# Summing a one-number-per-partition verdict: a one-column matmul against a GpSimd reduction, inside a matmul-bound kernel

## The chip, the cores and the metric

The kernel runs on one core of a Trainium2 chip. The metric is device time in microseconds (us), as a median of several executions. Engines are named as the profile names them: PE is TensorE (PEld its weight loads), DVE is VectorE, ACT is ScalarE, POOL is GpSimd, SP is SyncE.

## The reference

```python
batch, seq, dim, hidden = 16, 256, 512, 2048
def reference(x, w1, w2):
    h = x @ w1                              # 4096x512 @ 512x4096
    gate, value = np.split(h, 2, axis=-1)
    h = np.maximum(gate, 0) * value
    return (h @ w2).astype(np.float32)      # 4096x2048 @ 2048x512
```

## The kernel before

The kernel computes both matmuls in float16 with a seven-product (Strassen-like) scheme. This is only safe if the inputs have a normal scale. So the kernel sums squares of pieces of the inputs into a table `st` of 128 partitions by 152 columns, and during the last of its four second matmuls it judges the table. If every entry is between two bounds, a flag is 0 and the kernel ends; otherwise it does everything again in a general way. The steps that the change touches are these:

```python
    def judge():                                   # VectorE
        n = st.shape[1]
        ok = wpool.tile([P, n], F32, name="ok")
        fit = wpool.tile([P, 2], F16, name="fit")
        nc.vector.tensor_scalar(out=ok, in0=st, scalar1=HIGH, scalar2=None, op0=LE)
        nc.vector.scalar_tensor_tensor(out=ok, in0=st, scalar=LOW, in1=ok, op0=GE, op1=MULT)
        nc.vector.memset(fit, 1.0)
        with nc.allow_low_precision("whole numbers below 2048"):
            nc.vector.tensor_reduce(out=fit[:, :1], in_=ok, axis=mybir.AxisListType.X, op=ADD)
        return fit

    def count(fit):                                # TensorE, then VectorE
        n = P * st.shape[1]
        ps = psx.tile([P, TH], F32, name="X", tag="X")
        nc.tensor.matmul(ps[:1, :1], fit[:, :1], fit[:, 1:], start=True, stop=True)
        nc.vector.tensor_scalar(out=flag, in0=ps[:1, :1], scalar1=n - 0.5, scalar2=None, op0=LT)
# ... cut ...
            # the last second matmul is a stream of 112 steps, two matmuls each;
            # job(u, f) puts f ahead of step u
            job(18, lambda: verdict.append(judge()))
            job(46, lambda: count(verdict[0]))
            job(78, lambda: verdict.append(nc.values_load(flag[0:1, 0:1], ...)))   # every engine reads the flag
```

The other party in the story is a sum of two operands on VectorE, done sixteen times in the last stream. TensorE waits for these sums:

```python
    def sum_of(o, n, eng=nc.vector):
        i0, i1, op = SUMS_X[n]
        eng.tensor_tensor(o[n], o[i0], o[i1], op=op)     # 128x1024 float16, both inputs in SBUF
```

## Time and profile before

| | before |
|---|---|
| median time (first three runs) | 307.98 us |
| span of the profiled run | 305.6 us |
| TensorE busy | 300.7 us, 98% |
| VectorE, ScalarE, GpSimd busy | 77%, 58%, 49% |
| chain that ended last | 96% TensorE |
| one product of eight 128x256 matmuls | every 0.87 us |
| the product that holds the count | 1.08 us |

These lines are from the page of the kernel before: span, busy times, the granted clock in tenths in 40 slices, and the chain of waits that ended last.

```profile
span 305.6 us, 5338 instructions
PE 300.7 (98%) x1933; PEld 187.0 (61%) x1933; DVE 236.0 (77%) x388; ACT 176.5 (58%) x348; POOL 151.2 (49%) x189
PEclk9999999999999999999999999999999999999999
PE 96%; DMA 1%; SPq 0%; POOL 0%; ACT 0%; issue 0%
```

Nearly all of the span is TensorE, at full clock. Time is only gained where TensorE works less or waits less.

Next is the timeline of the kernel before around the count. The columns are start, duration, engine, line, operation and count of merged instructions; the bracket tells how long the engine was idle and what released it.

```profile
286.90 0.60 PE L369 MATMUL Y<-v_T,w_stage 128*128 128x256 f16 x4
287.43 0.08 PEld L675 LDWEIGHTS <-fit 128*1 128x1 f16 x1 [0.21 <-issue]
287.43 0.16 PE L675 MATMUL X<-fit 128*1 128x1 f16 x1
287.53 0.61 PE L369 MATMUL Y<-v_T,w_stage 128*128 128x256 f16 x4
287.71 0.14 DVE L676 TENSOR_SCALAR flag<-X 1x1 int32<-1x1 f32 x1
287.98 1.04 PE L369 MATMUL W<-w,w_stage 128*128 128x256 f16 x8
```

The starts matter here, since the ends of matmuls are modelled and overlap. From 286.90 to 287.98 us is 1.08 us, where a product takes 0.87 us. So the count costs TensorE 0.21 us. Ordinary weight loads start about 0.1 us ahead of their matmul; the load of `fit` starts together with it.

The listing by tile of the kernel before shows who reads the flag, and when ("first to last start" after the durations; the rows of the other engines' sequencers are left out).

```profile
L783 POOLq TENSOR_LOAD <-flag x1: 491/491/491, 287.9 to 287.9; - x1
L783 PEldq TENSOR_LOAD <-flag x1: 488/488/488, 292.6 to 292.6; - x1
```

The flag is ready at about 287.85 us. TensorE's sequencer only asks for it at 292.6 us.

### The profile page before, as it was taken

What the parts mean: (1) busy time and instruction counts of PE and PEld (TensorE: products, weight loads), DVE (VectorE), ACT (ScalarE), POOL (GpSimd) and SP (SyncE); (2) the same over time, 40 slices, a digit from 0 to 9 for tenths busy, and PEclk for the clock granted to TensorE, in tenths of its full rate; (3) what the DMA queues carried; (4) which work ended last, traced back from release to release, by engine and by line L of the source; (5) the groups of instructions that cost most, each with busy time, mean ns of one, the idle gap of its engine ahead of it and who ended that gap; (6) DMA issues with size and microseconds to landing.
All of it is one profiled execution on the core that took longest, in us unless ns stands there. A gap on an engine that the chain in (4) does not pass through costs nothing.

```text
span 305.6 us, 5338 instructions
## 1 busy us (share of the span) xinstructions
PE 300.7 (98%) x1933; PEld 187.0 (61%) x1933; DVE 236.0 (77%) x388; ACT 176.5 (58%) x348; POOL 151.2 (49%) x189
## 2 busy tenths in 40 slices
PE   8999999999999999999999999999999999999995
PEld 6854545688844444478864444458884444447884
DVE  2779888899768898887537888888546888888851
ACT  2588886455955555538855555545866555553231
POOL 2399999800069999300029989800006998800000
PEclk9999999999999999999999999999999999999999
DMA  7977679954794170001354910000325110000133
GB/s 236 356 233 219 213 176 177 223 114 87 266 200 92 64 138 3 0 2 63 136 175 108 206 36 2 0 2 2 138 91 185 35 34 2 1 1 27 45 105 107
DMA packets 35838, 32.89 MB, mean 108 GB/s; under 512 B 14432, under 2 KB 31328, under 8 KB 35680
## 3 DMA queue, kind: packets, MB, share of 16 engines
q1 hardware_dynamic: 33536, 26.22, 28.7%
q0 software_dynamic: 2272, 6.29, 11.6%
q8 instruction: 16, 0.26, 0.3%
q14 instruction: 14, 0.11, 0.1%
HBM read 27.26 MB, written 12.58 MB: 130 GB/s over the span
## 4 chain that ended last, share of the span: by engine, by line
PE 96%; DMA 1%; SPq 0%; POOL 0%; ACT 0%; issue 0%
PE Y L256 26%; PE W L256 18%; PE X L256 18%; PE Y L369 14%; PE X L369 9%; PE W L369 9%; DMA w_stage<-in_w_dram 1%; PE W L332 1%; PE X L332 1%; PE Y L332 1%; PE Y L511 0%; PE X L511 0%; SPq L501 0%; POOL w_T L479 0%; SPq L222 0%; ACT o L417 0%
## 5 line engine op out<-in xcount | busy, mean ns | idle before, releaser
L256 PEld LDWEIGHTS <-w_T 128*128 128x128 f16 x524 | 51.1, 98 | 54.6 <-POOL w_T L237 0.9
L184 POOL TENSOR_TENSOR fold<-xh 128x1024 f32<-128x1024 f16 x16 | 30.3, 1896 | 94.6 <-DMA xh<-x 93.7
L256 PE MATMUL X<-x_A,w_B 128*128 128x512 f16 x248 | 73.7, 379 | 0.0
L256 PE MATMUL Y<-x_S,w_T 128*128 128x512 f16 x220 | 65.4, 379 | 0.0
L256 PEld LDWEIGHTS <-w_B 128*128 128x128 f16 x372 | 36.4, 98 | 42.0
L284 DVE SCALAR_TENSOR_TENSOR cc<-W,pu 128x512 f32<-128x512 f32 x62 | 42.9, 692 | 21.3 <-ACT pu L278 21.3
L264 ACT COPY Y<-X 128x512 f32<-128x512 f32 x62 | 35.4, 571 | 38.2 <-PE X L256 37.9
L278 ACT ACTIVATE pu<-Y 128x512 f32<-128x512 f32 x62 | 37.1, 598 | 33.9 <-PE Y L256 32.9
L187 POOL TENSOR_TENSOR fold<-fold 128x512 f32<-128x512 f32 (+2 forms) x96 | 51.8, 540 | 7.5
L369 PEld LDWEIGHTS <-w_stage 128*128 128x128 f16 x512 | 50.0, 98 | 5.8
L294 DVE SCALAR_TENSOR_TENSOR cc<-Y,pu 128x512 f32<-128x512 f32 x62 | 42.9, 691 | 6.6
L289 DVE SCALAR_TENSOR_TENSOR g<-X,cc 128x512 f16<-128x512 f32 x62 | 42.9, 691 | 2.3
L306 DVE SCALAR_TENSOR_TENSOR g<-Y,cc 128x512 f16<-128x512 f32 x62 | 42.3, 682 | 1.8 <-PE Y L256 1.8
L369 PEld LDWEIGHTS <-g 128*128 128x128 f16 x384 | 37.5, 98 | 8.2
L271 ACT ACTIVATE pu<-W 128x512 f32<-128x512 f32 x62 | 37.2, 600 | 0.8 <-PE W L256 0.6
L256 PE MATMUL W<-x_S,w_T 128*128 128x512 f16 (+1 forms) x152 | 36.9, 340 | 0.0
L256 PE MATMUL W<-x_S,w_B 128*128 128x512 f16 x124 | 36.9, 379 | 0.0
L256 PE MATMUL Y<-x_A,w_T 128*128 128x512 f16 x124 | 36.9, 379 | 0.0
L369 PE MATMUL X<-w,g 128*128 128x256 f16 x256 | 31.9, 273 | 0.0
L405 DVE SCALAR_TENSOR_TENSOR o<-W,pu 128x256 f32<-128x256 f32 x16 | 6.8, 423 | 21.0 <-PE W L369 21.0
L174 DVE TENSOR_TENSOR w_stage<-g 128x1024 f16<-128x1024 f16 x32 | 21.4, 685 | 0.2
L237 POOL TENSOR_TENSOR w_T<-w_stage 128x512 f16<-128x512 f32 (+1 forms) x16 | 18.7, 1173 | 2.6 <-DMA w_stage<-in_w_dram 2.5
(100 smaller groups left out, 306.7 us busy)
## 6 DMA issues: line engine op xcount, KB each, us to landing
w_stage<-in_w_dram SPq DMA_DIRECT2D x14, 512.0 KB, 6.0
out_dram<-o SPq DMA_DIRECT2D x26, 256.0 KB, 2.2
x<-in_x_dram POOLq DMA_DIRECT2D x4, 1024.0 KB, 10.5
xh<-x SPq DMA_DIRECT2D x16, 256.0 KB, 3.2
w<-in_w_dram POOLq DMA_DIRECT2D x2, 1024.0 KB, 10.0
out_dram<-o SPq DMA_DIRECT2D x12, 128.0 KB, 1.7
w_stage<-in_w_dram SPq DMA_DIRECT2D x4, 256.0 KB, 4.8
x_S<-in_x_dram SPq DMA_DIRECT2D x4, 256.0 KB, 5.7
```

The lines of the kernel that those rows point to most:

```text
L174: eng.tensor_tensor(o[n], o[i0], o[i1], op=op)
L184: nc.gpsimd.tensor_tensor(fold, t, t, op=MULT)
L187: nc.gpsimd.tensor_tensor(fold[:, :, :m], fold[:, :, :m], fold[:, :, m:2 * m], op=ADD)
L256: nc.tensor.matmul(ps[:, slice(*c)], wop[wn][:, b, self.jb * P:(self.jb + 1) * P], self.xo[xn][:, b, slice(*c)], start=fresh and b == c[0] ...
L264: nc.scalar.copy(out=self.Y, in_=self.X)
L271: nc.scalar.activation(self.p5, self.W, COPY, scale=GS)
L278: nc.scalar.activation(self.u2, self.Y, COPY, scale=GS)
L284: nc.vector.scalar_tensor_tensor(out=self.c12, in0=self.W, scalar=GS, in1=self.u2, op0=MULT, op1=ADD)
L289: nc.vector.scalar_tensor_tensor(out=self.g[:, self.jb, :TH], in0=self.X, scalar=0.0, in1=self.c12, op0=MAX, op1=MULT)
L294: nc.vector.scalar_tensor_tensor(out=self.c22, in0=self.Y, scalar=GS, in1=self.p5, op0=MULT, op1=ADD)
L306: nc.vector.scalar_tensor_tensor(out=self.g[:, self.jb, TH:], in0=self.Y, scalar=0.0, in1=self.c22, op0=MAX, op1=MULT)
L369: nc.tensor.matmul(ps, self.op[an][:, i], vop[wn][:, i], start=name in ("P1", "P5") and i == 0, stop=i == NJ // 2 - 1, skip_group_check=True)
```

## The change

The intent is to take the count from TensorE, which is the bottleneck, and give it to GpSimd, which is idle from 266.9 us on.

```diff
-        fit = wpool.tile([P, 2], F16, name="fit")
+        fit = wpool.tile([P, 1], F32, name="fit")
         ...
-        nc.vector.memset(fit, 1.0)
-        with nc.allow_low_precision("whole numbers below 2048"):
-            nc.vector.tensor_reduce(out=fit[:, :1], in_=ok, axis=mybir.AxisListType.X, op=ADD)
+        nc.vector.tensor_reduce(out=fit, in_=ok, axis=mybir.AxisListType.X, op=ADD)
@@ def count(fit):
-        ps = psx.tile([P, TH], F32, name="X", tag="X")
-        nc.tensor.matmul(ps[:1, :1], fit[:, :1], fit[:, 1:], start=True, stop=True)
-        nc.vector.tensor_scalar(out=flag, in0=ps[:1, :1], scalar1=n - 0.5, scalar2=None, op0=LT)
+        total = wpool.tile([1, 1], F32, name="total")
+        nc.gpsimd.tensor_reduce(out=total, in_=fit, axis=mybir.AxisListType.C, op=ADD)
+        nc.gpsimd.tensor_scalar(out=flag, in0=total, scalar1=n - 0.5, scalar2=None, op0=LT)
@@
-            job(46, lambda: count(verdict[0]))
+            job(18, lambda: count(verdict[0]))
```

## The prediction

> **What bounds the kernel.** TensorE. The page gives PE 300.7 us of a 305.6 us span (98%) at a granted clock of nine tenths or more in every slice, and the chain that ended last is 96% PE. VectorE is at 77%, ScalarE 58%, GpSimd 49%. Only what TensorE does, or waits for, costs time.
>
> **Where the change sits.** In the last second matmul. The timeline shows the verdict made on VectorE from 283.07 us (two compares, a memset of 0.06 us, a 0.31 us reduction ending at about 284.5 us). At 287.43 us TensorE does the one-column weight load (79 ns) and matmul (164 ns); VectorE compares at 287.71 us (0.14 us). The listing by tile shows who reads the flag: GpSimd's sequencer at 287.9 us, TensorE's at 292.6, ScalarE's at 293.4, VectorE's at 294.4, SyncE's at 295.2.
>
> **What is removed.** A product of eight matmuls goes by every 0.87 us (284.28, 285.16, 286.03, 286.90); the one with the count in it takes 1.08 us (286.90 to 287.98). So the count costs TensorE about 0.21 us, also seen as a 0.21 us "issue" gap before its weight load. This lies on the chain, so about 0.2 us comes back. VectorE loses 0.20 us (memset and compare), off the chain: it idles 1.3 to 2.1 us at a time here. One use of an X bank goes too; the next product into X starts at 294.09 us without a wait, so that gives nothing.
>
> **What is added.** On GpSimd, idle from 266.9 us on apart from its flag load: a sum of 128x1 over the partitions and a 1x1 compare. The trace has no sum over partitions. The Trainium skill ("GPSIMD Engine Reference", section "Cross-partition — where GPSIMD wins") states 247.7 us for 128x2048; no run here shows it yet. That is 0.12 us a column, if it goes column by column; with the 0.2 us of a small GpSimd instruction here (128x8 add, 203 ns) I estimate 0.5 to 3 us for the sum, say 1.5 us, and 0.1 to 0.2 us for the compare. The same page (section "Instruction dispatch") puts some 6 us on the first call into freshly loaded code; nothing shows that this needs it.
>
> **What of it is critical.** The sum can start at about 284.6 us. TensorE's sequencer asks for the flag at 292.6 us, and TensorE has queued work until about 294.5 us (the load sits inside the product that starts at 294.09 us). So sum plus compare may take about 8 us before the sequencer waits, about 9 before the matmuls do. At 1.5 us the flag comes at about 286.4 us, earlier than before. I expect no wait. GpSimd could hinder VectorE's 128x1024 sums that feed TensorE, but over the whole run these took 678 to 693 ns with GpSimd busy half the time, and the new instruction reads only 128 numbers.
>
> **Prediction.** 307.98 - 0.2 = 307.8 us; the runs of before alone scatter by 1 us. Range 307.1 to 308.7. Faster by over 2%: 0.01; within 2%: 0.92; slower by over 2%: 0.07.
>
> **What would show it right.** No one-column matmul; all products around 287 us 0.87 us apart; a GpSimd sum of 1 to 3 us starting near 284.6 us; no gap in PE after TensorE's flag load; the chain still 96% PE; the 128x1024 sums still 0.69 us.
>
> **What would make it wrong.** A sum with a fixed cost above 8 us (TensorE then stalls by the excess, one for one; over about 14 us it is 2% slower); a compare that reads the total too early, so that the general way runs and the time jumps by far more; or a long GpSimd instruction that holds VectorE's sums back.

## The result, and the profile after

The first measurement gave 308.37 us (307.63 to 308.71, 6 runs) for the changed kernel and 307.86 us (307.52 to 308.58, 6 runs) for the kernel before. The ratio is 1.0006, 95% interval 0.9987 to 1.0026: the same. A ratio is the mean time of one kernel's fast runs over that of the other's of the same rounds, so it is not quite the ratio of the medians. The result was correct, and the prediction's range (307.1 to 308.7) held it. That is no test of the 0.2 us: the range is wider than the scatter, and would have held a change that does nothing.

The page of the changed kernel:

```profile
span 305.4 us, 5336 instructions
PE 300.2 (98%) x1932; PEld 186.5 (61%) x1932; DVE 235.9 (77%) x386; ACT 176.5 (58%) x348; POOL 152.6 (50%) x191
PE 96%; DMA 1%; SPq 0%; POOL 0%; ACT 0%; issue 0%
```

The timeline of the changed kernel over the same work (rows of other instructions left out):

```profile
284.42 0.68 DVE L174 TENSOR_TENSOR w_stage<-g 128x1024 f16<-128x1024 f16 x1
...
284.58 0.74 POOL L673 CROSS_LANE_REDUCE total<-fit 128x1 f32<-128x1 f32 x1 [17.50 <-DVE fit L655]
285.13 0.69 DVE L174 TENSOR_TENSOR w_stage<-w_stage,g 128x1024 f16<-128x1024 f16 x1
...
285.41 0.50 POOL L674 TENSOR_SCALAR flag<-total 1x1 int32<-1x1 f32 x1
...
286.93 1.04 PE L369 MATMUL Y<-v_T,w_stage 128*128 128x256 f16 x8
...
287.81 1.04 PE L369 MATMUL W<-w,w_stage 128*128 128x256 f16 x8
```

The product of 286.93 us is whole again, and the next one follows 0.88 us later, not 1.08. The GpSimd sum took 0.74 us, the compare 0.50 us. The flag's readers:

```profile
L781 POOLq TENSOR_LOAD <-flag x1: 492/492/492, 285.9 to 285.9; - x1
L781 PEldq TENSOR_LOAD <-flag x1: 485/485/485, 292.4 to 292.4; - x1
```

The flag is ready at 285.9 us, two microseconds earlier than before and 6.5 us before TensorE's sequencer asks. TensorE doesn't wait for it.

A gain of 0.21 us can't be seen in times that scatter by 1 us. It can be seen inside one profile, as the length of the last stream. The measure used below is the time from the start of the last pair of first-matmul instructions to the start of the last product. Here are the two ends, first of the kernel before, then of the changed kernel:

```profile
279.05 0.59 PE L256 MATMUL Y<-x_A,w_T 128*128 128x512 f16 x2
301.08 1.04 PE L369 MATMUL Y<-v_T,g 128*128 128x256 f16 x8
```

```profile
279.08 0.59 PE L256 MATMUL Y<-x_A,w_T 128*128 128x512 f16 x2
300.90 1.04 PE L369 MATMUL Y<-v_T,g 128*128 128x256 f16 x8
```

| profile | from | to | last stream (difference) |
|---|---|---|---|
| before | 279.05 | 301.08 | 22.03 us |
| after | 279.08 | 300.90 | 21.82 us |
| after_again | 279.38 | 301.21 | 21.83 us |
| sums8 | 279.65 | 301.48 | 21.83 us |
| sums24_late | 279.96 | 301.79 | 21.83 us |
| whole | 279.50 | 301.32 | 21.82 us |
| no_verdict | 279.89 | 301.72 | 21.83 us |
| square1 | 279.36 | 301.21 | 21.85 us |
| square16 | 279.78 | 302.01 | 22.23 us |
| counts32_together | 279.48 | 302.29 | 22.81 us |
| spread16 | 279.44 | 304.49 | 25.05 us |

All kernels without a count on TensorE agree to 0.01 us, 0.20 to 0.21 us below the kernel before. (The other labels are the experiments below.) (counts32_spread, sums24 and wide are left out: TensorE stood still in their last stream, which took 37.60, 28.80 and 31.25 us.) The arrival at this stage, in the column "from", varies by 0.9 us between profiles in which everything up to there is the same work. It isn't the verdict that moves it.

### The profile page after: what moved, and what is told of

Its sections match the earlier page's. It is cut to its first block, busy times and chain, and to the rows that moved or that the text cites. A ratio compares the mean times of both kernels' runs of the same rounds, so it can differ in the third digit from the quotient of the medians.

```text
span 305.4 us, 5336 instructions
## 1 busy us (share of the span) xinstructions
PE 300.2 (98%) x1932; PEld 186.5 (61%) x1932; DVE 235.9 (77%) x386; ACT 176.5 (58%) x348; POOL 152.6 (50%) x191
## 4 chain that ended last, share of the span: by engine, by line
PE 96%; DMA 1%; SPq 0%; POOL 0%; ACT 0%; issue 0%
PE Y L256 26%; PE W L256 18%; PE X L256 18%; PE Y L369 14%; PE X L369 9%; PE W L369 9%; DMA w_stage<-in_w_dram 1%; PE W L332 1%; PE X L332 1%; PE Y L332 1%; PE Y L511 0%; PE X L511 0%; SPq L501 0%; POOL w_T L479 0%; SPq L222 0%; ACT o L417 0%
## 5 line engine op out<-in xcount | busy, mean ns | idle before, releaser
L405 DVE SCALAR_TENSOR_TENSOR o<-W,pu 128x256 f32<-128x256 f32 x16 | 6.8, 423 | 20.5 <-PE W L369 20.5
```

## The experiments

The theory: the count costs TensorE 0.21 us because its odd weight load breaks the stream of hidden loads; GpSimd's sum is hidden because some 9 us pass before the flag is missed. Rivals: the gap is a wait paid once, or a bare slot of the matmul; the slack is not there; GpSimd's work hinders VectorE; the change costs time somewhere outside the profiled stage.

### after_again: the changed kernel once more

No edit.

> The changed kernel once more, with more runs. My theory: the 0.21 us that TensorE gets back is there in every run, but the single runs of both kernels fall near 307.6 or near 308.6 us, so a median of few runs says nothing of it; ratio to before between 0.998 and 1.001, with runs of both kernels in both groups. Rival: the change costs time outside the profiled stretch (the medians so far say +0.5 us); then the changed kernel has clearly more runs near 308.6 and a ratio above 1.001.

Measured: 307.97 us (307.76 to 308.24, 5 runs) against 308.11 us (307.67 to 308.48, 9 runs); ratio 0.9997 (0.9983 to 1.0011). The rival, a cost outside the stage, falls: the +0.5 us between the first medians didn't return. The split into two groups of times that I expected wasn't there either; the runs of both kernels spread evenly. Times can't tell whether the 0.21 us were gained; the stage length can.

### counts32_spread and counts32_together: 32 counts in place of one

```diff
# counts32_spread: the count's matmul, into one bank, ahead of each of the steps 24 to 55; compare after the last
+            for u in range(24, 55):
+                job(u, lambda: count_once(verdict[0]))
-            job(46, lambda: count(verdict[0]))
+            job(55, lambda: count(verdict[0]))
# counts32_together: all at the old place
+        for _ in range(32):
             nc.tensor.matmul(ps[:1, :1], fit[:, :1], fit[:, 1:], start=True, stop=True)
```

> The kernel before with 32 one-column matmuls in place of one, one after every second matmul of the last second matmul, all ahead of the compare. My theory: each takes a slot of TensorE and interrupts the stream of hidden weight loads, about 0.21 us each, so 32 of them 6.6 us longer than before less nothing else (31 x 0.21 = 6.5 us; 314.4 us, ratio 1.021). Rival A: only the first costs 0.21 us because it waits for something once (its input or its bank), the others about 0.1 us for the bare slot: +3.3 us. Rival B: the gap was not of the count: below +1 us.

> The same 32 one-column matmuls, all at the place of the one. If half of the 0.21 us is an interruption of the stream paid once, and half a slot of about 0.1 us per matmul, this costs 0.1 + 31 x 0.1 = 3.2 us, half of the spread version; if each costs 0.21 us wherever it stands, 6.5 us as spread.

Measured, together: 308.76 us (4 runs), ratio 1.0028 (1.0012 to 1.0043), +0.65 us by the medians. The timeline shows all 32 as one group:

```profile
287.87 0.94 PE L676 MATMUL X<-fit 128*1 128x1 f16 x32
288.74 2.08 PEld L369 LDWEIGHTS <-w_stage 128*128 128x128 f16 x20
```

From 287.87 to the next ordinary work at 288.74 us are 0.87 us for 32 counts, 0.027 us each. So the matmul itself is nearly free, and neither a slot of 0.1 us nor 0.21 us apiece is right: the price is for entering and leaving the odd form once. The stage length says the same: 22.81 us is 0.99 us more than without a count, which is 0.20 us once and 31 times 0.025.

Measured, spread: 323.5 us (4 runs), ratio 1.0493 (1.0476 to 1.0509), +15.4 us. This is far above both expectations, and the granted clock of the run was 0.967. The table by stretches shows why (the columns are the stretch, busy us and instructions of PE, PEld, DVE, ACT and POOL, then the granted clock, the DMA share and GB/s; the rows from 290 to 306 us, all at 0.50, are left out):

```profile
283.00:285.00 2.00, 0.30 (x3) 0.02 (x1) 1.97 (x7) 0.39 (x1) 0.00 (x0) 1.00 0.17 58
285.00:287.00 2.00, 1.86 (x14) 0.94 (x15) 1.93 (x4) 0.01 (x1) 0.00 (x0) 1.00 0.00 0
287.00:290.00 3.00, 3.00 (x15) 0.93 (x15) 0.14 (x1) 0.75 (x2) 0.00 (x0) 0.50 0.00 0
306.00:308.00 2.00, 2.00 (x14) 1.48 (x13) 0.83 (x2) 0.54 (x2) 0.00 (x0) 0.63 0.38 119
308.00:312.00 4.00, 4.00 (x39) 3.60 (x37) 1.47 (x3) 1.35 (x4) 0.00 (x0) 1.00 0.16 54
```

Two things were mixed. I had put the first count at step 24, where the verdict wasn't ready, so TensorE stood still for 1.84 us. And from about 287 to 307.5 us the granted clock was 0.50 (the mean of 0.63 from 306 to 308 us is three quarters of it at 0.50). The first counts after the standstill still cost 0.20 us each (a group of two matmuls and a count took 0.42 us, two matmuls alone take 0.22); at half clock a group took 0.63 us. (The 0.41 us a count that the next expectation names for half clock is reckoned against two matmuls at full clock. At half clock two take 0.43 us, a quarter of a product's 1.70, so a count still cost 0.20 us there.) Whether the standstill or the interruptions brought the clock down needed another run. As an estimate from these numbers, 1.84 us of standstill and 31 counts at 0.20 us make 8.0 of the 15.4 us; the rest is the half clock.

### spread16 and square16: interruptions without a standstill, and without the odd weight load

```diff
# spread16: as counts32_spread, steps 40 to 55, where the verdict has long been ready
-            for u in range(24, 55):
+            for u in range(40, 55):
# square16: as spread16, but a matrix of ones (set by GpSimd long before) is the weight
-        nc.tensor.matmul(counts[0][:1, :1], fit[:, :1], fit[:, 1:], start=True, stop=True)
+        nc.tensor.matmul(counts[0][:, :1], ones, fit[:, :1], start=True, stop=True)
```

> Sixteen one-column matmuls in the kernel before, one after every second matmul, starting where the verdict has long been ready, so that TensorE never waits for it. In the run with 32 each cost 0.20 us (0.42 us for a group of two matmuls and a count, against 0.22 us for the two alone) until the granted clock fell to 0.50 at about 287 us, and 0.41 us after. Theory A: the clock fell because TensorE stood still for 1.84 us for the first count; then here the clock stays at 1.0 and the run is 15 x 0.20 = 3.0 us longer than before. Theory B: the interruptions themselves bring the clock down; then the clock falls to 0.5 within the 6.7 us of the stretch, and the run is 5 us or more longer.

> The same sixteen counts at the same places, but with a 128x128 matrix of ones as the weights and the one column as the moving operand, so that the weight load has the form of all others. My theory: the 0.2 us is weight loads that are not hidden, because the one-column load does not start ahead of the running matmul and neither does the load after it; a full-width load is hidden, so each count costs 0.03 to 0.11 us: 0.5 to 1.8 us longer than before and no fall of the clock. Rival: any stray matmul of one moving column costs 0.2 us; then as spread16.

Measured: spread16 311.12 us against 308.11 us (ratio 1.0097, 1.0080 to 1.0114), that is +3.01 us for 15 more counts, 0.20 us each, at a clock of 1.0. Theory B falls: sixteen interruptions over 6.7 us didn't bring the clock down. That the standstill did it alone, as theory A says, is not shown: no run has one of 1.84 us in the stream without interruptions after it. In the start-up of the run no_verdict, told below, TensorE stood still for 1.48 us (5.83 to 7.31 us) and the granted clock stayed at 1.00. The two together, in counts32_spread, remain a possible cause. square16 took 308.5 us (ratio 1.0008, 0.9991 to 1.0025). The timelines of PE show the difference, first spread16:

```profile
287.36 0.16 PE L675 MATMUL X<-fit 128*1 128x1 f16 x1
287.45 0.39 PE L369 MATMUL W<-v_T,w_stage 128*128 128x256 f16 x2
287.78 0.16 PE L675 MATMUL X<-fit 128*1 128x1 f16 x1
```

then square16, with the weight load of its count:

```profile
287.25 0.17 PE L675 MATMUL X<-fit,ones 128*128 128x1 f16 x1
287.28 0.38 PE L369 MATMUL W<-v_T,w_stage 128*128 128x256 f16 x2
287.39 0.10 PEld L675 LDWEIGHTS <-ones 128*128 128x128 f16 x1
287.50 0.17 PE L675 MATMUL X<-fit,ones 128*128 128x1 f16 x1
```

One group takes 0.42 us in spread16 and 0.25 us in square16. With full-width weights the load starts at 287.39 us, 0.11 us ahead of its matmul, behind the running matmuls, and the count costs 0.025 us: sixteen lengthen the stage from 21.83 to 22.23 us. With the one-column weight neither its load nor the next one is hidden. So the 0.21 us belongs to the form of the weight load. Which property of that form does it (its width, or that it is not of the same form as its neighbours) was not tried by a run of its own; but in counts32_together 32 one-column loads in a row went by every 0.027 us, which speaks against the width alone and for the change of form.

### sums8, sums24 and sums24_late: how much slack the flag has

```diff
# sums8, sums24: the sum repeated
+        for _ in range(8):        # 24 in sums24 and sums24_late
             nc.gpsimd.tensor_reduce(out=total, in_=fit, axis=mybir.AxisListType.C, op=ADD)
# sums24_late, in addition
-            job(78, lambda: verdict.append(nc.values_load(
+            job(108, lambda: verdict.append(nc.values_load(
```

> The changed kernel with its sum over the partitions done eight times in a row, about 0.8 us each by the profile: the flag would come at 284.6 + 8 x 0.83 + 0.5 = 291.7 us, still before TensorE's sequencer asks for it at 292.4 us. My theory (there are 8 us of slack): no change of time against the changed kernel, no gap in PE. Rival (GpSimd's work holds back VectorE or the flag is needed earlier): 1 us or more longer, with VectorE's 128x1024 sums longer than 0.69 us.

> The changed kernel with its sum over the partitions done 24 times in a row, 0.60 us each as the run with eight measured: the flag comes at 284.8 + 24 x 0.60 + 0.56 = 299.8 us. My theory (the matmuls run dry about 2 us after TensorE's sequencer asks at 292.5 us, at 294.5 us): TensorE stands still from about 294.5 to 300.3 us, 5.5 to 6 us longer, unless the standstill also halves the clock afterwards, which would add 1 to 4 us. Rival (the flag is only needed at the end, by the branch): no change.

> The same 24 sums, with the flag loaded 30 steps later in the last stream (step 108 of 112 in place of 78). By my theory TensorE's sequencer then asks at about 299 us and its matmuls run dry at about 301 us, after the flag has come: no change against the kernel before (within 0.3%). If the wait were a matter of GpSimd's work as such, as long as sums24.

Measured: sums8 307.8 us (ratio 0.9987, 0.9972 to 1.0002), no wait; the eight sums took 0.60 us each in place of the 0.83 that I had assumed, so the flag came at 290.6 us. sums24 took 314.86 us against 308.11 us (ratio 1.0206, 1.0180 to 1.0231), +6.75 us, at a granted clock of 0.987 to 0.995. sums24_late took 308.57 us (ratio 1.0008, 0.9991 to 1.0024), with the stage at 21.83 us. The timelines of GpSimd and of PE in sums24:

```profile
285.24 13.40 POOL L674 CROSS_LANE_REDUCE total<-fit 128x1 f32<-128x1 f32 x24 [17.57 <-DVE fit L655]
298.73 0.23 POOL L675 TENSOR_SCALAR flag<-total 1x1 int32<-1x1 f32 x1
```

```profile
294.58 0.60 PE L369 MATMUL X<-w,g 128*128 128x256 f16 x4
299.52 1.01 PE L369 MATMUL X<-w,g 128*128 128x256 f16 x4 [4.34 <-POOL flag L675]
300.32 1.91 PE L369 MATMUL Y<-w,w_stage 128*128 128x256 f16 x8
302.03 1.91 PE L369 MATMUL Y<-v_T,w_stage 128*128 128x256 f16 x8
303.74 1.47 PE L369 MATMUL W<-v_T,w_stage 128*128 128x256 f16 x8
```

Four matmuls started at 294.58 us and the fifth would have followed at about 295.02; it came at 299.52 us, 4.50 us late. The flag came at 298.96 us, so it could have come at about 294.5 us without harm: the slack was some 9.2 us from 285.24 us, as predicted. But the loss isn't one for one. The products that start at 300.32 and 302.03 us take 1.71 us each, half speed; by 305.05 us this had cost another 2.5 us (5.53 us for 28 matmuls, which take 3.05 us at 0.109 us each). Moving the load 30 steps later made the same 24 sums free. That shows that the cost was the wait for the flag, not GpSimd's work.

### wide and whole: what the number of columns costs

```diff
# wide: one more sum over the partitions ahead of the real one, result unused
+        cols = wpool.tile([1, st.shape[1]], F32, name="cols")
+        nc.gpsimd.tensor_reduce(out=cols, in_=ok, axis=mybir.AxisListType.C, op=ADD)
# whole: no VectorE reduction; GpSimd sums the whole table to one number
-        nc.vector.tensor_reduce(out=fit, in_=ok, axis=mybir.AxisListType.X, op=ADD)
-        return fit
+        return ok          # so count's argument fit is now the table
-        nc.gpsimd.tensor_reduce(out=total, in_=fit, axis=mybir.AxisListType.C, op=ADD)
+        nc.gpsimd.tensor_reduce(out=total, in_=fit, axis=mybir.AxisListType.XYZWC, op=ADD)
```

> The changed kernel with one more sum over the partitions, of the whole 128x152 table of verdicts, ahead of the sum of 128x1; its result is not used. The prediction took 0.12 us a column from the Trainium skill's 247.7 us for 128x2048. If that holds for 152 columns, this sum takes 18 us, the flag comes at 284.2 + 18.3 + 0.6 + 0.5 = 303.6 us, TensorE stands still from 294.6 to 304 us and runs at half clock for some 5 us after, so 11 to 12 us longer. If the time is a fixed cost with little per column (a 128x1 sum took 0.56 to 0.60 us in a row), no change of time and a sum of about 1 us.

> The changed kernel without VectorE's reduction: GpSimd sums the 128x152 table over columns and partitions in one instruction. It is slower than 8 us if the cost goes by columns (then the kernel is longer by more than its time minus 9 us), and has no effect on the kernel's time if below 8 us. VectorE loses 0.31 us, which is worth nothing.

Measured: wide 316.85 us against 308.23 us (ratio 1.0271, 1.0243 to 1.0299), +8.6 us where I expected 11 to 12, at a granted clock of 0.988 to 0.989. The timelines of GpSimd, VectorE and PE in wide:

```profile
284.41 17.02 POOL L675 CROSS_LANE_REDUCE cols<-ok 128x152 f32<-128x152 f32 x1 [17.56 <-DVE ok L654]
```

```profile
284.59 8.53 DVE L174 TENSOR_TENSOR w_stage<-g 128x1024 f16<-128x1024 f16 x1
293.15 0.69 DVE L174 TENSOR_TENSOR w_stage<-w_stage,g 128x1024 f16<-128x1024 f16 x1
```

```profile
285.36 1.04 PE L369 MATMUL Y<-w,w_stage 128*128 128x256 f16 x8
293.18 1.89 PE L369 MATMUL W<-v_T,w_stage 128*128 128x256 f16 x8 [6.78 <-DVE w_stage L174]
```

The size was right: 17.02 us for 152 columns, 0.11 us a column. The mechanism of the loss was not the one that I expected. TensorE didn't wait for the flag at 294 us. It waited from 286 us on for VectorE, whose two-input sum, started 0.18 us after GpSimd's reduction, took 8.53 us in place of 0.69. After that TensorE again ran three products at half clock (1.70 us each).

whole, in one untimed look: correct, 307.99 us, the stage at 21.82 us.

```profile
284.65 1.25 POOL L671 CROSS_LANE_REDUCE total<-ok 128x1 f32<-128x152 f32 x1 [17.42 <-DVE ok L653]
```

GpSimd summed 128x152 numbers to one in 1.25 us, fourteen times faster than to 152 sums (part of the 1.25 us may be a wait: one of VectorE's two-input sums ran until 285.18 us). The branch of my expectation in which the cost goes by columns falls: it goes by results, it seems. One of VectorE's sums took 0.85 us in this run, which cost nothing.

### square1 and no_verdict: what is there to gain

```diff
# square1: the kernel before, its one count in the full-width form
-        nc.tensor.matmul(ps[:1, :1], fit[:, :1], fit[:, 1:], start=True, stop=True)
+        nc.tensor.matmul(ps[:, :1], ones, fit[:, :1], start=True, stop=True)
# no_verdict: the changed kernel without judge and count (right for these inputs only)
-            job(18, lambda: verdict.append(judge()))
-            job(18, lambda: count(verdict[0]))
+            verdict.append(None)
+            job(18, lambda: nc.gpsimd.memset(flag, 0))
```

> The kernel before with its one count in the form with 128x128 weights of ones. By the run with sixteen such counts each adds 0.025 us: the product with the count in it takes about 0.90 us in place of 1.08, the gap in the weight loads is gone, and 0.18 of the 0.2 us comes back without GpSimd. The time itself: same as before and as the change within 0.2%.

> The changed kernel without the verdict: the flag is set to zero by GpSimd (right for these inputs only). It bounds what any change of the verdict's last step can give. My theory: the verdict is off the chain, so the time is within 0.2% of the changed kernel's and no more than 0.3 us below the kernel before's. Rival: the waits for the flag or VectorE's four verdict instructions cost something; then 1 us or more shorter.

Measured: square1 307.72 us (ratio 0.9983, 0.9956 to 1.0009), no_verdict 307.84 us (ratio 0.9983, 0.9957 to 1.0009), against 308.23 us. Neither is distinguishable from the kernel before by its time (no_verdict's median is 0.39 us below, a little more than the 0.3 that I allowed, but the interval of the ratio includes 1). By the stage, square1 takes 21.85 us and no_verdict 21.83 us. So taking the verdict away altogether gives no more than the change did, and the matmul in another form gives all but 0.02 to 0.03 us of it. No version beat the kernel before clear of the noise.

Where the noise sits can be read in the first 10 us. Here are rows of PE's timeline, first of before, then of no_verdict, whose last stream began 0.84 us later:

```profile
7.19 0.39 PE L332 MATMUL W<-x_A,w_T 128*128 128x256 f16 x2 [0.20 <-POOL w_T L479]
```

```profile
7.31 0.61 PE L332 MATMUL X<-x_A,w_B 128*128 128x256 f16 x4 [1.48 <-POOL w_B L479]
```

In the start-up TensorE waits for GpSimd's first casts, which wait for the first loads of weights, in no_verdict 1.3 us longer in all (1.48 us against 0.20), of which 0.84 us is left at the last stream. These two profiles show it; that it explains the scatter of all runs is argued, not shown.

## Why the prediction was right, point by point

- **TensorE bounds the kernel, and the count costs it 0.21 us.** Right. The stage went from 22.03 to 21.82 us, and 15 more counts of the same form cost 0.20 us each. The predicted ratio, 307.8 over 307.98 or 0.9994, lies within the 95% intervals of both measurements, but so does 1: the times alone don't show the gain.
- **The sum takes 0.5 to 3 us, say 1.5, and the compare 0.1 to 0.2 us.** The range held; the guess within it was high, and the list of what would show it right named 1 to 3 us, which was missed. The sum took 0.74 us in the changed kernel and 0.36 us where nothing disturbed it (the median of the 24). The compare took 0.50 us, outside my range; undisturbed it took 0.23 us. In both cases the longer time ends just after a two-input sum of VectorE ends (285.10 and 285.82 us in the changed kernel; the GpSimd instructions end at 285.32 and 285.91 us). This points to VectorE delaying GpSimd, where I had only asked about the reverse. The 24 sums of sums24, looked up one by one in the trace, bear it out: nine began while one of VectorE's two-input sums ran (one of the nine at its start, to within 0.01 us) and took 0.53 to 0.90 us; the other fifteen took 0.36 us. No run was made for it alone.
- **About 8 us before the sequencer waits, 9 before the matmuls do.** Right: 9.2 us by sums24; with 24 sums GpSimd was busy 13.7 us and the kernel 2.06% slower, near the "over about 14 us". That nearness is luck: one for one beyond 9.2 us, 13.7 us would cost 4.5 us, or 1.5%; the rest is the half clock, which the prediction didn't have.
- **TensorE then stalls by the excess, one for one.** Wrong in size, on a path that the change didn't take: 4.5 us of standstill cost 6.75 us, because half clock followed.
- **GpSimd doesn't hinder VectorE's sums.** Right for this kernel (they kept to 0.69 us), but the reason given was weak. That they took 678 to 693 ns over the whole run "with GpSimd busy half the time" says nothing: in the trace of the kernel before none of these 64 sums overlaps a GpSimd instruction. A 17 us reduction stretched one to 8.53 us. What saves the change, by these runs, is that its instruction is short: in sums24 one of VectorE's sums began at 289.95 us, while a GpSimd sum of 0.36 us ran (289.70 to 290.06 us), and was not held back (0.68 us). The Trainium skill ("SBUF — State Buffer", section "Who interferes with whom") says that VectorE instructions with two SBUF inputs contend with GpSimd instructions that read SBUF and that the loser blocks; reading that page would have given the right reason. The trace of wide agrees (8.53 us in place of 0.69).
- **The first-call cost of some 6 us in the Trainium skill ("GPSIMD Engine Reference", section "Instruction dispatch").** It was not seen: the first and only sum took 0.74 us.

## What to carry to other kernels

Taking a small operation off the bottleneck engine is worth what it costs there, read from the starts of its neighbours, and here this was 0.2 us of 308, one fifth of the scatter of runs; measure such a gain as the length of a stage in the profile, and by multiplying the operation. Before moving work, ask whether another form makes it free where it is: the same count with full-width weights cost 0.025 us in place of 0.2. On the new engine, check two deadlines: when the result is first missed (and that TensorE's standstills of 4.5 and 6.8 us here were paid for again at half clock), and which instructions of other engines the operation holds back while it runs.

## What the Trainium skill lacked or had wrong

- "TensorE: Matmul & The Clock Gate", step ① of "Step-by-step: what each phase is for", says that weight loads are pulled ahead of running matmuls. It lacks that a one-column load between full ones is not, nor the load after it: 0.20 us each time here, against 0.025 us for a 128-column load, and against 0.027 us for a one-column load among 31 others.
- The same page, Part 1, gives about 3.4 us of idling for the fall to half clock. Here the clock fell to 0.50 in counts32_spread after a standstill of only 1.84 us and five interruptions, and stayed there for 20.5 us, 17.3 of them with an interruption in every 0.63 us, although the trace shows matmuls throughout. In sums24 and wide, without interruptions, it fell some 2.7 and 5.0 us into the standstill and stayed there for 6.8 us. Sixteen interruptions without a standstill left it at 1.0 for 6.7 us, and so did a standstill of 1.48 us in a start-up (no_verdict). Which of the two matters how much is open.
- "GPSIMD Engine Reference", section "Cross-partition — where GPSIMD wins", has one figure, 247.7 us for 128x2048, or 0.12 us a column. This case agrees (17.02 us for 152 columns) and adds what the page lacks: 0.36 us for one column, and 1.25 us for a whole 128x152 table into one number.
- "SBUF — State Buffer", section "SBUF: two separate sides", says that the shared port pair is held for the whole instruction. In wide VectorE's sum was blocked for 7.8 us (8.53 less 0.69), but sums of the same kind then ran in 0.69 us while GpSimd's reduction is still on record to 301.4 us. So the block ended about half way through the instruction, as far as GpSimd's recorded span can be trusted (its next instruction starts only at 301.40 us).
